# A two-layer hybrid block in fp32: every pair of the up-projection in seven products, its sums of h formed from the transposes, the modulation in single steps

## The chip, the cores and the metric

The kernel runs on one core of one Trainium2 chip. The metric is the device time of one execution in microseconds. The engines have these names in the profile: PE is the matmul engine (PEld its weight loads), DVE the vector engine, ACT the scalar engine, POOL is GpSimd, and SP the engine whose queue issues the DMAs here. SBUF is the on-chip memory in which the kernel keeps its tiles, PSUM the banks into which PE writes. All sizes are fp32: a 128x512 tile is 256 KB.

## What is computed

Two layers on 1024 tokens of width 1024, batch 1. Each layer has a mixer of three parallel branches and an MLP of width 4096. Six vectors from a condition, the modulation, scale and shift the two normalised inputs and gate the two outputs.

```python
cond = jax.nn.silu(c)
for l in range(DEPTH):
    mod = (cond @ w_ada[l] + b_ada[l])[:, None, :]
    sh_m, sc_m, g_m, sh_f, sc_f, g_f = jnp.split(mod, 6, axis=-1)
    h = _rmsnorm(x, norm_g[l, 0]) * (1.0 + sc_m) + sh_m
    y = _hybrid_mixer(h, ...)
    x = x + g_m * _rmsnorm(y, norm_g[l, 1])
    h = _rmsnorm(x, norm_g[l, 2]) * (1.0 + sc_f) + sh_f
    y = jnp.square(jax.nn.relu(h @ w_up[l])) @ w_down[l]
    x = x + g_f * _rmsnorm(y, norm_g[l, 3])
```

The change is in `h @ w_up` (1024x1024 by 1024x4096), in what leads up to it, and in the places at which the modulation is worked out.

## The kernel before

**Products.** Every fp32 operand is split into a high part (fp32r) and a remainder (`split`: a cast on ACT at L199, a subtraction on DVE at L200). A product is three matmuls: high by high (L192), high by low (L193), low by high (L194). The split arrays lie in numbered slots of one tile, named `split` in the profile; fp32 buffers come from an arena, named `arena_f`.

**Layout.** h is kept transposed: features on partitions in eight blocks of 128, tokens along the free dimension, as a high array hh and a low array hl. `B(k, n)` is a quarter of it: four feature blocks (k) by 512 tokens (n). A product of 12 matmuls takes four feature blocks of 128 weights by 512 tokens.

**The up-projection** (`mlp_up`) takes the 32 blocks of 128 hidden features in pairs. Fourteen pairs are done in seven products instead of eight, each 2x2 block problem by sums: the products use B(0,0), B(1,0), B(1,1) and four sums of quarters of h, T0 to T3; the weights are summed alike on POOL and split (`forms`, `cut`), and DVE adds the products up (L316-334). The first four blocks, f = 0 to 3, are done plainly, in 24 matmuls for each half of the tokens, 192 in all. They give the time in which the T sums are formed from hh and hl (`form`): each of the four sums has four blocks, each with two subtractions (L248, L249), an addition (L250) and a split. Three sums are on DVE and T2 on POOL. A later sum needs an earlier one: T1 needs T0, T3 needs T1. Then follow 14 x 7 x 12 = 1176 matmuls. The sums of weights reuse the slots of the second token half of h, one ring of four.

**What comes ahead.** The output projection's last two token tiles, out(6) and out(7), are woven with the second norm of tiles 0 to 5 (`renorm`: a norm whose last addition is on POOL at L596, eight transposes on PE at L604, a cast and a subtraction at L606 and L607). The norms of tiles 6 and 7 are a generator, `late`, that `mlp_up` drains between the halves of its first two plain blocks.

**The down-projection** (`mlp_down`) reads the squared hidden blocks back from memory (d_r) in nine groups of 2, 4, 4, 4, 4, 4, 4, 2 and 4 blocks, with eight token tiles each. In the last group `finish` adds the residual of a token tile and, in layer 0, starts the next layer's norm and transposes (L612).

**The modulation** is worked out in chunks of 128 columns: 512 KB of w_ada, eight multiply-adds of 128x128 on DVE (L535), a matmul with ones (L546), and a small store. A generator, `bg`, is stepped at fixed places: once a pair in up, once a block in down, two chunks a step. It has 56 chunks behind layer 0's mixer and none behind layer 1's.

**Order.** A scheduler with a simulated timeline reorders the instructions when the program is built; on the chip each engine takes its own queue in that order, and the DMAs named above are all issued from SP's queue. So what is written in one place of the code may stand among others in a queue.

## Time and profile before

| | us |
|---|---|
| median of three runs | 2866.52 |
| lowest and highest | 2861.63, 2880.45 |
| the profiled execution | 2878.17 |
| its span, first to last instruction | 2876.5 |
| mean granted clock of PE | 0.946 |

The profiled execution is 11.65 us above the median; the prediction's durations are all from it. In the page, busy time of an engine is the sum of its instructions' durations, and a matmul's duration covers more than its share of a pipelined stream, so a pace is read from counts in a window of full load. "Idle before" is the time in which an engine waited, and the name behind the arrow is what ended it. The granted clock is the share of full speed that PE had. A line of this profile, such as L604, is five lines lower after the change from `mlp_up`'s end on (L609), since the code above it grew.

### The profile page before, as it was taken

The numbers are of one execution on the slowest core, as the hardware profiler recorded it, in microseconds if no ns is written. First come the engines' busy times: TensorE is split into PE (matmuls) and PEld (weight loads), VectorE is DVE, ScalarE is ACT, GpSimd is POOL, SyncE is SP. The second block draws the span as 40 slices with busy tenths as digits, with TensorE's granted clock in tenths as the row PEclk, the third lists the DMA queues.
The fourth block names the chain that finished last, engine by engine and source line by source line (L and its number), as shares of the span: only waits on it lengthen the run. The fifth ranks groups of instructions, "written<-read, shape, count | busy, mean of one in ns | idle before, by whom it ended". The sixth has DMA issues, their size and how long they took to land. (4 is left out here: it accounts for less than half of the span.)

```text
span 2876.5 us, 34698 instructions
## 1 busy us (share of the span) xinstructions
PE 2661.0 (93%) x12578; PEld 2078.7 (72%) x12578; DVE 1747.1 (61%) x3148; ACT 1098.4 (38%) x2105; POOL 665.7 (23%) x532
## 2 busy tenths in 40 slices
PE   5799998999789998999988999999987999999998
PEld 4677776676667776678867877666766788788886
DVE  7767677543878667764365585664448655543435
ACT  5233444544344444212142443454443555621212
POOL 1341244201532220000042113341016432100002
PEclk9899989899899999999998998899998999999999
DMA  6441213312255455643141121132131433541303
GB/s 222 115 132 56 86 59 95 100 58 87 65 165 168 135 164 168 213 155 117 43 138 42 55 83 64 60 110 77 51 118 51 139 114 110 176 149 60 117 30 117
DMA packets 257231, 306.80 MB, mean 107 GB/s; under 512 B 25442, under 2 KB 200740, under 8 KB 257060
## 3 DMA queue, kind: packets, MB, share of 16 engines
q1 hardware_dynamic: 257060, 304.59, 32.9%
q8 instruction: 99, 1.62, 0.2%
q14 instruction: 72, 0.59, 0.1%
HBM read 238.11 MB, written 66.43 MB: 106 GB/s over the span
## 5 line engine op out<-in xcount | busy, mean ns | idle before, releaser
L192 PE MATMUL bank_b<-split 128*128 128x512 f32 (+2 forms) x1840 | 736.1, 400 | 44.1 <-ACT split L199 24.1
L194 PE MATMUL bank_b<-split 128*128 128x512 f32 (+2 forms) x1840 | 716.6, 390 | 7.5 <-DVE split L200 6.5
L193 PE MATMUL bank_b<-split 128*128 128x512 f32 (+2 forms) x1840 | 718.2, 390 | 0.4 <-DVE split L651 0.3
L199 ACT CAST split<-arena_f 128x512 fp32r<-128x512 f32 (+1 forms) x364 | 274.3, 778 | 748.5 <-PE bank_s L193 360.0
L192 PE MATMUL bank_s<-split 128*128 128x512 f32 (+2 forms) x1152 | 455.6, 399 | 29.2 <-ACT split L199 12.6
L193 PE MATMUL bank_s<-split 128*128 128x512 f32 (+2 forms) x1152 | 453.7, 394 | 9.1 <-DVE split L200 5.9
L194 PE MATMUL bank_s<-split 128*128 128x512 f32 (+2 forms) x1152 | 450.3, 391 | 0.0
L192 PEld LDWEIGHTS bank_b<-split 128*128 128x128 f32 x1840 | 358.1, 195 | 125.3 <-ACT split L199 25.8
L194 PEld LDWEIGHTS bank_b<-split 128*128 128x128 f32 x1840 | 356.5, 194 | 79.6 <-DVE split L200 9.3
L193 PEld LDWEIGHTS bank_b<-split 128*128 128x128 f32 x1840 | 358.4, 195 | 68.1 <-issue 4.5
L200 DVE TENSOR_TENSOR split<-arena_f,split 128x512 fp32r<-128x512 f32 (+1 forms) x356 | 334.9, 956 | 111.7 <-ACT split L199 111.5
L375 DVE TENSOR_TENSOR arena_f<-arena_f,bank_s 128x1024 f32<-128x1024 f32 x128 | 155.9, 1218 | 269.8 <-PE bank_s L194 269.8
L192 PEld LDWEIGHTS bank_s<-split 128*128 128x128 f32 (+1 forms) x1152 | 219.4, 191 | 84.5 <-ACT split L199 15.3
L193 PEld LDWEIGHTS bank_s<-split 128*128 128x128 f32 (+1 forms) x1152 | 220.8, 192 | 58.8 <-DVE split L200 9.6
L194 PEld LDWEIGHTS bank_s<-split 128*128 128x128 f32 (+1 forms) x1152 | 220.6, 192 | 44.1 <-issue 1.0
L825 DVE TENSOR_REDUCE nm<-bank_s 128x1 f32<-128x128 f32 (+3 forms) x192 | 141.7, 751 | 125.4 <-PE bank_s L1040 65.2
L826 ACT ACTIVATE arena_f<-bank_s,nm 128x128 f32<-128x128 f32 (+4 forms) x192 | 141.9, 741 | 189.3 <-DVE nm L825 163.9
L535 DVE SCALAR_TENSOR_TENSOR arena_f<-arena_f,cond 128x128 f32<-128x128 f32 x448 | 163.9, 394 | 65.4 <-DMA arena_f<-in_w_ada 28.7
L625 POOL TENSOR_TENSOR arena_f<-arena_f 128x1024 f32<-128x1024 f32 x16 | 43.7, 2731 | 596.9 <-DVE arena_f L624 593.8
L891 PE MATMUL bank_s<-split 32*128 32x512 f32 (+3 forms) x576 | 117.3, 383 | 12.1 <-ACT arena_f L826 9.8
L854 ACT COPY arena_f<-bank_t 128x512 f32<-128x512 f32 (+1 forms) x160 | 86.7, 542 | 104.9 <-PE bank_t L851 94.5
L838 PE MATMUL bank_a<-arena_f 128*64 128x256 f32 (+1 forms) x640 | 108.4, 398 | 13.6 <-ACT arena_f L854 12.1
(277 smaller groups left out, 3286.6 us busy)
## 6 DMA issues: line engine op xcount, KB each, us to landing
arena_f<-in_w_ada SPq DMA_DIRECT2D x80, 512.0 KB
d_r<-arena_f SPq DMA_DIRECT2D x128, 256.0 KB
arena_f<-in_w_down SPq DMA_DIRECT2D x64, 512.0 KB
arena_f<-d_r SPq DMA_DIRECT2D x64, 512.0 KB
arena_f<-in_w_up SPq DMA_DIRECT2D x28, 1024.0 KB
arena_f<-d_x SPq DMA_DIRECT2D x36, 512.0 KB
d_x<-arena_f SPq DMA_DIRECT2D x24, 512.0 KB
arena_f<-in_w_in SPq DMA_DIRECT2D x20, 512.0 KB
```

Of the source, the lines that this page charges most:

```text
L192: mm(out, wh, xh, start=start, stop=False)
L193: mm(out, wh, xl, start=False, stop=False)
L194: mm(out, wl, xh, start=False, stop=stop)
L199: self.nc.scalar.copy(hi, src)
L200: (eng or self.nc.vector).tensor_sub(lo, src, f32(hi))
L375: nc.vector.tensor_add(y[t], y[t], ps)
L535: nc.vector.scalar_tensor_tensor(acc, in0=w[:, k], scalar=self.cond[:, k:k + 1], in1=acc, op0=ALU.mult, op1=ALU.add)
L825: nc.vector.tensor_reduce(nm, S[:, 0:n], axis=AX.X, op=ALU.max, negate=True)
L826: nc.scalar.activation(p[:, 0:n], S[:, 0:n], AF.Exp, bias=nm, accum_out=ls)
L838: nc.tensor.matmul(bk[jj * 64:jj * 64 + 64, 128 * half:256], v[:, 2 * c + jj], e[:, 256:384] if half else e[:, jj * 256:jj * 256 + 256], s ...
L854: nc.scalar.copy(held, ps[:, 0:w])
L891: nc.tensor.matmul(S[mp][:, c0:c1], Q[rw, a, tok], K[rw, b, c0:c1], start=a == b, stop=a == 1 and c1 < n)
```

## The change

All 16 pairs are done in seven products. For the first six (`LEAD`) the two products that need no sum, B(0,0) and B(1,0), run first: they need the tokens 0 to 511 alone. The first of the two is kept in the arena until the pair's other five products. From the seventh pair on, all seven stand together. The plain blocks and `form` go.

The norms of tiles 4 to 7 are `late` now, two steps of it ahead of each lead pair, and the weave ahead has tiles 0 to 3 alone. For tiles 4 to 7, `transp_late` takes the place of `transp8`: POOL adds the high and low parts of the first token half (two additions, L208), PE transposes (L211), and DVE forms the four sums of a tile from the transposes' PSUM, each fp32 sum split at once into its columns of T0 to T3 (four subtractions, L217, and five splits, L230 and L231). The weights of the first six pairs are read a second time for their second part.

A step of the modulation's generator is one chunk instead of two; up has two steps a pair, down one after every second token tile of groups 1 to 6 and after every tile of group 7, and none in groups 0 and 8. In the last group of down in layer 0, the next layer's norm of a tile comes a tile earlier and its transposes one tile earlier, so one deferred norm instead of two is left behind the last tile.

Counts: 24 matmuls of 128x512 fewer in each layer. Three places show what moves in the queues.

DVE in layer 0, before, from the last late norm on (L595 the norm, L607 the remainders of two transposed tiles; L248 to L250 and L200 the sums T and their splits):

```order
L595 SCALAR_TENSOR_TENSOR arena_f<-arena_f,rstd_y_5864 128x1024
L607 TENSOR_TENSOR split<-bank_s,split 128x8x128 x2
L248 TENSOR_TENSOR arena_f<-split 128x512 x4
L249 TENSOR_TENSOR arena_f<-split 128x512 x4
L250 TENSOR_TENSOR arena_f<-arena_f 128x512 x4
L200 TENSOR_TENSOR split<-arena_f,split 128x512
L248 TENSOR_TENSOR arena_f<-split 128x512
```

DVE in layer 0, after, between the norm of the last tile (L600) and the sums of that tile (L217, L231; L307 adds two products, L540 is the modulation's multiply-add):

```order
L600 SCALAR_TENSOR_TENSOR arena_f<-arena_f,rstd_y_5960 128x1024
L231 TENSOR_TENSOR split<-arena_f,split 128x512 x2
L540 SCALAR_TENSOR_TENSOR arena_f<-arena_f,cond 128x128 x4
L307 TENSOR_TENSOR arena_f<-arena_f,bank_b 128x512
L540 SCALAR_TENSOR_TENSOR arena_f<-arena_f,cond 128x128 x7
L217 TENSOR_TENSOR arena_f<-bank_s,arena_f 128x512
L540 SCALAR_TENSOR_TENSOR arena_f<-arena_f,cond 128x128
L217 TENSOR_TENSOR arena_f<-bank_s,arena_f 128x512
L540 SCALAR_TENSOR_TENSOR arena_f<-arena_f,cond 128x128
L231 TENSOR_TENSOR split<-arena_f,split 128x4x128
L217 TENSOR_TENSOR arena_f<-arena_f 128x512 x2
L540 SCALAR_TENSOR_TENSOR arena_f<-arena_f,cond 128x128
```

The sums stand by token tile now, with the modulation's multiply-adds ahead of and among those of the last tile.

PE in layer 0, before: the transposes of the last two tiles stand together, between plain products.

```order
L192 MATMUL bank_b<-split 128x512
L193 MATMUL bank_b<-split 128x512
L604 MATMUL bank_s<-ident,arena_f 128x128 x16
L192 MATMUL bank_b<-split 128x512 x2
L193 MATMUL bank_b<-split 128x512
```

PE in layer 0, after, at the third of four such places, between lead products:

```order
L193 MATMUL bank_b<-split 128x512
L194 MATMUL bank_b<-split 128x512
L211 MATMUL bank_s<-ident,arena_f 128x128 x8
L192 MATMUL bank_b<-split 128x512
L193 MATMUL bank_b<-split 128x512
```

The transposes of tiles 4 to 7 are spread over the lead, a tile at a time.

SP's queue in layer 0, before, at the third and fourth load for the down-projection (L345 reads w_down and the hidden blocks, L520 w_ada, L218 stores hidden blocks):

```order
L520 DMA arena_f<-in_w_ada 128x8x128
L345 DMA arena_f<-in_w_down 128x1024
L520 DMA arena_f<-in_w_ada 128x8x128
L345 DMA arena_f<-in_w_down 128x1024
L520 DMA arena_f<-in_w_ada 128x8x128
L218 DMA d_r_109<-arena_f 128x512
L557 DMA d_mod<-arena_f 1x128
L526 DMA arena_f<-in_b_ada 1x128
L218 DMA d_r_109<-arena_f 128x512
L531 DMA arena_f<-in_norm_g 1x128
L520 DMA arena_f<-in_w_ada 128x8x128
L218 DMA d_r_109<-arena_f 128x512
```

The same place after (L349, L525 and L248 are those three; L644 reads w_in for the next layer):

```order
L349 DMA arena_f<-in_w_down 128x1024
L349 DMA arena_f<-d_r_109 128x1024
L349 DMA arena_f<-in_w_down 128x1024
L349 DMA arena_f<-d_r_109 128x1024
L562 DMA d_mod<-arena_f 1x128
L248 DMA d_r_109<-arena_f 128x512
L531 DMA arena_f<-in_b_ada 1x128
L525 DMA arena_f<-in_w_ada 128x8x128
L644 DMA arena_f<-in_w_in 128x2x128 x2
L525 DMA arena_f<-in_w_ada 128x8x128
L644 DMA arena_f<-in_w_in 128x2x128
L248 DMA d_r_109<-arena_f 128x512
```

Between the third and the fourth load of w_down stands no w_ada now; from the third to the sixth there are three of them where there were six.

```diff
@@ -29,9 +29,9 @@
 OFF = 0, 0, 0.1, 2
 OUTS = (), (0, 1), (2, 3), (4, 5)
 WOW = 16
-LAG = 4
 NVEC = 6
 GROUPS = [2] + [4] * 6 + [2, 4]
+LEAD = 6
 C_Q, C_K, C_V, C_CQ, C_CKV, C_KR, C_Z, C_XBC, C_DT = 0, 256, 512, 768, 1024, 1152, 1184, 1696, 2464
 
 SLOT = 2048
@@ -194,6 +194,37 @@
         mm(out, wl, xh, start=False, stop=stop)
 
 
+    def sums(self):
+
+        return [self.slot(2 * n, 2, 4, 512) for n in range(4)]
+
+    def transp_late(self, x, hT, t):
+
+        nc, F = self.nc, self.F
+        T = self.sums()
+        tok, sl = slice(t * P, t * P + P), slice((t - 4) * P, (t - 3) * P)
+        b = [F.get(4, P) for _ in range(2)]
+        for n in range(2):
+            nc.gpsimd.tensor_add(b[n], *(f32(h[:, n * 4:n * 4 + 4, sl]) for h in hT))
+        ps = self.bank2()
+        for k in range(KD):
+            nc.tensor.transpose(ps[:, k * P:k * P + P], x[:, k * P:k * P + P], self.ident)
+        pv = ps.rearrange("p (n k q) -> p n k q", n=2, q=P)
+
+        def put(n, a, c):
+
+            e = F.get(4, P)
+            nc.vector.tensor_sub(e, a, c)
+            self.split(e, *(T[n][:, m, :, sl] for m in range(2)))
+            return e
+
+        e1 = put(0, pv[:, 0], b[0])
+        e2 = put(1, pv[:, 1], e1)
+        e3 = put(2, e2, b[0])
+        self.split(pv[:, 1], *(h[:, 4:8, tok] for h in hT))
+        e4 = put(3, b[1], e2)
+        F.put(e1, e2, e3, e4, *b)
+
     def split(self, src, hi, lo, eng=None):
 
         self.nc.scalar.copy(hi, src)
@@ -212,91 +243,47 @@
 
         def store(f, hf, t):
 
-            r = F.get(512) if t.tensor is not self.F.t.tensor else t
-            nc.scalar.activation(r, t, AF.Relu)
-            nc.scalar.activation(r, r, AF.Square)
-            dma(self.d_r[l][f, :, half[hf]], r)
-            F.put(r)
-
...
+            nc.scalar.activation(t, t, AF.Relu)
+            nc.scalar.activation(t, t, AF.Square)
+            dma(self.d_r[l][f, :, half[hf]], t)
+            F.put(t)
+
+
+        ring = [tuple(h[:, k, half[1]].rearrange("p (k f) -> p k f", f=P) for h in hT) for k in range(4)]
+        turn = [0]
+
+        def cut(src):
+            r = ring[turn[0] % 4]
+            turn[0] += 1
+            self.split(src, *r)
+            return r
+
+        def forms(i, plain, sums):
+
+            n = 2 * P if sums else P
+            st = F.get(KD, n)
+            dma(st, w_up[:, :, i * 2 * P:i * 2 * P + n])
+            a11, a12 = st[:, 0:4, 0:P], st[:, 4:8, 0:P]
+            if plain:
+                yield cut(a11)
+                yield cut(a12)
+            if sums:
+                a21, a22 = st[:, 0:4, P:2 * P], st[:, 4:8, P:2 * P]
+                s1, s2 = F.get(4, P), F.get(4, P)
+                nc.gpsimd.tensor_add(s1, a21, a22)
+                nc.gpsimd.tensor_sub(s2, s1, a11)
+                yield cut(s2)
+                nc.gpsimd.tensor_sub(a21, a11, a21)
+                yield cut(a21)
+                yield cut(s1)
+                nc.gpsimd.tensor_sub(s2, a12, s2)
+                yield cut(s2)
+                F.put(s1, s2)
+                yield cut(a22)
             F.put(st)
...
         N = FF // (2 * P)
-        parts = self.chain(*(forms(i) for i in range(2, N)))
+        parts = self.chain(*(forms(i, True, False) for i in range(LEAD)), *(forms(i, i >= LEAD, True) for i in range(N)))
         queue = [next(parts) for _ in range(3)]
 
         def product(b):
@@ -310,18 +297,24 @@
             return ps
 
         add = nc.vector.tensor_add
-        for i in range(2, N):
-            f = 2 * i
-            ps, p1 = product(B(0, 0)), F.get(512)
-            nc.scalar.copy(p1, ps)
+        T = [tuple(t[:, a] for a in range(2)) for t in self.sums()]
+        p1 = {}
+
+        def plain(i):
+            ps, p = product(B(0, 0)), F.get(512)
+            nc.scalar.copy(p, ps)
             ps, c = product(B(1, 0)), F.get(512)
-            add(c, p1, ps)
-            store(f, 0, c)
-            ps, u2 = product(part(1)), p1
-            add(u2, p1, ps)
-            ps, u3 = product(part(2)), F.get(512)
+            add(c, p, ps)
+            store(2 * i, 0, c)
+            p1[i] = p
+
+        def sums(i):
+            f, p = 2 * i, p1.pop(i)
+            ps, u2 = product(T[1]), p
+            add(u2, p, ps)
+            ps, u3 = product(T[2]), F.get(512)
             add(u3, u2, ps)
-            ps = product(part(0))
+            ps = product(T[0])
             add(u2, u2, ps)
             c = F.get(512)
             add(c, u3, ps)
@@ -329,9 +322,20 @@
             ps = product(B(1, 1))
             add(u2, u2, ps)
             store(f, 1, u2)
-            ps = product(part(3))
+            ps = product(T[3])
             add(u3, u3, ps)
             store(f + 1, 0, u3)
+
+        for i in range(LEAD):
+            next(late, None)
+            next(late, None)
+            plain(i)
+        self.drain(late)
+        for i in range(N):
+            if i >= LEAD:
+                plain(i)
+            sums(i)
+            next(bg, None)
             next(bg, None)
 
     def mlp_down(self, l, y, bg, finish):
@@ -360,7 +364,6 @@
             rw = []
             for f in fs:
                 rw.append((load(self.d_r[l][f]), load(w_dn[f * P:(f + 1) * P, :])))
-                next(bg, None)
             for t in range(NT):
                 tok = slice(t * P, t * P + P)
                 ps = self.bank2()
@@ -375,6 +378,8 @@
                     nc.vector.tensor_add(y[t], y[t], ps)
                 if last:
                     finish(t)
+                elif g and t % 2 or g == len(GROUPS) - 2:
+                    next(bg, None)
             for (i, _), (k, _) in rw:
                 free.extend((i, k))
 
@@ -1275,7 +1280,10 @@
         self.norm(x, *nxt, u)
         F.put(x)
         yield 1.0
-        self.transp8(u, hT[0], hT[1], t, True)
+        if t < 4:
+            self.transp8(u, hT[0], hT[1], t, True)
+        else:
+            self.transp_late(u, hT, t)
         F.put(u)
         yield 1.0
 
@@ -1303,9 +1311,9 @@
         nxt = self.mod_load(l, 4), self.mod_load(l, 3)
         kept = {}
         self.weave((26, self.chain(out(6, own(6), kept), out(7, own(7), kept))),
-                   (14, self.chain(*(self.renorm(t, dst, nxt, hT) for t in range(6)))))
+                   (9, self.chain(*(self.renorm(t, dst, nxt, hT) for t in range(4)))))
         yield
-        yield from self.chain(*(self.renorm(t, kept, nxt, hT) for t in (6, 7)))
+        yield from self.chain(*(self.renorm(t, dst if t < 6 else kept, nxt, hT) for t in range(4, NT)))
         F.put(g, *nxt)
 
     @staticmethod
@@ -1458,18 +1466,18 @@
                         tail["w"] = list(self.stage_w(I["w_in"][l + 1], self.qk_cols(0), 2))
                 if more and t == NT - 1:
                     tail["w0"] = self.load_w(tail["w"], 2)
-                if more and LAG - 1 < t < NT:
-                    self.transp8(y[t - LAG], hT[0], hT[1], t - LAG)
-                    F.put(y[t - LAG])
+                if more and 2 < t < 7:
+                    self.transp8(y[t - 3], hT[0], hT[1], t - 3)
+                    F.put(y[t - 3])
+                if more and 0 < t <= NT:
+                    self.norm(tail["x"][(t - 1) % 3], *tail["nxt"], y[t - 1], nc.vector if t > NVEC else nc.gpsimd)
                 if t < NT:
                     self.finish(y[t], self.d_x[2 * l], tail["g"], o, t, tail["x"][t % 3], y[t],
                                 hT[0][:, :, t * P:t * P + P])
-                if more and t > 1:
-                    self.norm(tail["x"][(t - 2) % 3], *tail["nxt"], y[t - 2], nc.vector if t > NVEC else nc.gpsimd)
 
             bg = iter(())
             if more:
-                bg = self.mod_stream(self.mod_rows(0, (5,) if l == 0 else (), 128) + self.mod_rows(l + 1, range(6), 128), 2)
+                bg = self.mod_stream(self.mod_rows(0, (5,) if l == 0 else (), 128) + self.mod_rows(l + 1, range(6), 128), 1)
             with self.phase(t=1, b=3):
                 self.mlp_up(l, hT, bg, late)
             with self.phase(t=2, b=2):
@@ -1479,9 +1487,8 @@
                 F.put(tail["g"])
                 if more:
                     finish(NT)
-                    finish(NT + 1)
                     F.put(*tail["nxt"])
-                    for t in range(NT - LAG, NT):
+                    for t in range(4, NT):
                         self.transp8(y[t], hT[0], hT[1], t, True)
                         F.put(y[t])
                         yield
```

60 lines of the change are left out of this document (removed).

## The prediction

> **What bounds the kernel now.** I read the page first, for the busy shares and the chain that ended last.
>
> ```profile
> PE 2661.0 (93%) x12578; PEld 2078.7 (72%) x12578; DVE 1747.1 (61%) x3148; ACT 1098.4 (38%) x2105; POOL 665.7 (23%) x532
> PE 32%; DVE 4%; ACT 1%; DMA 1%; issue 1%; POOL 1%; POOLq 0%; SPq 0%; DVEq 0%; ACTq 0%
> ```
>
> PE is busy for 93% of the span, so time is won either by fewer matmuls or in the places where PE waits or runs slowly. The windows find those places. Their columns are the stretch, its length, busy time and count of PE, weight loads, DVE, ACT and POOL, then the granted clock, the DMA share and GB/s.
>
> ```profile
> 2260.00:2280.00 20.00, 20.00 (x90) 16.57 (x89) 11.75 (x15) 10.27 (x18) 7.77 (x5) 1.00 0.34 117
> 733.00:815.00 82.00, 56.86 (x229) 44.49 (x227) 68.43 (x99) 28.25 (x47) 46.62 (x27) 0.82 0.32 99
> ```
>
> The first row is the up-projection at full speed: 90 matmuls of 128x512 in 20 us, 0.222 us each. The second is a stretch that the change rebuilds, from the last matmul of the output projection to the first product of the pairs, in layer 0. Its ends, and those of layer 1, are in the timeline (start, duration, engine, line, what it works on, idle before it).
>
> ```profile
> 733.63 1.03 PE L604 MATMUL bank_s<-ident,arena_f 128*128 128x128 f32 x8
> 753.50 1.97 PE L604 MATMUL bank_s<-ident,arena_f 128*128 128x128 f32 x8 [3.56 <-POOL arena_f L596]
> 814.88 0.80 PE L192 MATMUL bank_b<-split 128*128 128x512 f32 x1 [10.72 <-ACT split L199]
> 2163.74 1.91 PE L604 MATMUL bank_s<-ident,arena_f 128*128 128x128 f32 x16
> 2234.84 0.50 PE L192 MATMUL bank_b<-split 128*128 128x512 f32 x1 [0.75 <-ACT split L199]
> ```
>
> Layer 0 spends 814.88 - 733.63 = 81.3 us and layer 1 71.1 us on 192 plain matmuls (192 x 0.222 = 42.6) and 24 transposes (about 3). The rest, 35 and 25 us, is waiting and half-speed matmuls. The waits of PE in 733 to 816 (total, times, longest) say on whom:
>
> ```profile
> PE bank_b L192 <- ACT split L199: 16.1, 2, 10.7
> PE bank_s L604 <- POOL arena_f L596: 5.0, 2, 3.6
> PE bank_b L194 <- DVE split L200: 2.9, 2, 2.2
> ```
>
> ACT is named, but only because its cast stands behind a DVE result: DVE makes three of the four sums of h, and is busy 68 of 82 us.
>
> **The lead: price of its parts.** Its durations come from DVE and POOL rows of the same stretch.
>
> ```profile
> 757.69 5.86 DVE L248 TENSOR_TENSOR arena_f<-split 128x512 f32<-128x512 f32 x4
> 763.47 6.86 DVE L249 TENSOR_TENSOR arena_f<-split 128x512 f32<-128x512 f32 x4
> 770.26 4.63 DVE L250 TENSOR_TENSOR arena_f<-arena_f 128x512 f32<-128x512 f32 x4
> 775.41 0.68 DVE L248 TENSOR_TENSOR arena_f<-split 128x512 f32<-128x512 f32 x1
> 776.01 0.68 DVE L200 TENSOR_TENSOR split<-arena_f,split 128x512 fp32r<-128x512 f32 x1
> 756.66 6.34 POOL L248 TENSOR_TENSOR arena_f<-split 128x512 f32<-128x512 f32 x4 [3.22 <-ACT split L606]
> 762.96 5.13 POOL L249 TENSOR_TENSOR arena_f<-split 128x512 f32<-128x512 f32 x3
> 768.06 5.07 POOL L250 TENSOR_TENSOR arena_f<-arena_f 128x512 f32<-128x512 f32 x3
> 790.40 1.27 POOL L249 TENSOR_TENSOR arena_f<-split 128x512 f32<-128x512 f32 x1
> 751.10 2.34 POOL L596 TENSOR_TENSOR arena_f<-arena_f 128x1024 f32<-128x1024 f32 x1 [4.66 <-DVE arena_f L595]
> 749.73 1.28 DVE L595 SCALAR_TENSOR_TENSOR arena_f<-arena_f,rstd_y 128x1024 f32<-128x1024 f32 x1
> 741.59 0.14 DVE L166 TENSOR_SCALAR rs_m<-fs 128x1 f32<-128x1 f32 x1
> 746.21 1.23 DVE L1258 TENSOR_TENSOR arena_f<-arena_f 128x1024 f32<-128x1024 f32 x1
> 756.55 1.22 DVE L607 TENSOR_TENSOR split<-bank_s,split 128x1024 fp32r<-128x1024 f32 x1 [4.04 <-ACT split L606]
> ```
>
> With POOL at rest a DVE operation of 128x512 follows the last after 0.60 us (775.41 to 776.01). The twelve operations from 757.69 to 774.9 took 17.2 us where 12 x 0.60 = 7.2 would do, and POOL worked 16.5 us of that time: each us of POOL cost DVE 10.0 / 16.5 = 0.6 us.
>
> The changed lead has 144 matmuls (six pairs, two products of 12) and 32 transposes. PE alone needs 144 x 0.222 + 4 x 1.03 = 36 us. On DVE, from the same start to the first product with a sum, the order has 36 operations of the T sums (4 tiles x 9), 8 cuts of weights and 6 adds of products, 50 x 0.60 = 30; three norms of 1.28 with a short chain each, 5.0 (an estimate); and the last tile's root, scale and add, 741.59 to 747.44 less an L607 of 1.1 that stands between, 4.7. Together 39.7 us. In layer 0 also 24 of the modulation's multiply-adds stand among them, 0.27 apiece (23 in 6.13 us, row below): 6.5, so 46.2. POOL in the same stretch has 8 new adds of 1.27 and three or four of 2.34: 18.4 us. DVE, not PE, sets the lead.
>
> Bounds: 46 (layer 0) and 40 (layer 1) if POOL costs DVE nothing; 46 + 18 = 64 and 40 + 18 = 58 if DVE stands still whenever POOL works, and beyond that the waits at the head of DVE's queue, of which layer 0 has those for the modulation's weights:
>
> ```profile
> 977.39 0.71 DVE L535 SCALAR_TENSOR_TENSOR arena_f<-arena_f,cond 128x128 f32<-128x128 f32 x1 [6.57 <-DMA arena_f<-in_w_ada]
> 981.50 0.77 PE L192 MATMUL bank_b<-split 128*128 128x512 f32 x1 [3.54 <-DVE arena_f L327]
> 980.00:1000.00 20.00, 18.50 (x69) 14.63 (x70) 12.84 (x26) 9.96 (x18) 2.62 (x3) 0.83 0.50 158
> 1132.06 6.13 DVE L535 SCALAR_TENSOR_TENSOR arena_f<-arena_f,cond 128x128 f32<-128x128 f32 x23 [1.90 <-DMA arena_f<-in_w_ada]
> ```
>
> The multiply-adds are queued ahead of the last tile's T sums, so one such wait of 6.57 delays the first product with a sum in full. I take the measured 0.6: 46.2 + 0.6 x 18.4 + 6.6 = 64 in layer 0, and 39.7 + 11 + 4 for the last tile's chain of row steps = 55 in layer 1 (in layer 0 before, DVE idled 4.04 us for the transposes of tile 7). **The leads give -17 (81.3 to 64) and -16 (71.1 to 55).** Far ends: 46 and 40, or 77 and 66, the full exclusion with two such waits or chains.
>
> The Trainium skill, page "SBUF — State Buffer", section "Who interferes with whom", says that a VectorE instruction with two SBUF inputs and a GpSimd instruction that reads SBUF exclude each other for the whole instruction, while VectorE with one SBUF input does not contend. This speaks against the new adds on GpSimd, and by it only the three of a tile's nine T operations that read PSUM escape. The trace agrees in direction: 17.2 us for 7.2 us of work, 0.6 of POOL's time and not all of it. The full exclusion is the second rival below.
>
> **The other parts.** The remaining main loop has 1200 matmuls where it had 1176: 24 x 0.222 = +5.3 in each layer, **+10.7**; the PE stream as a whole loses 2 x 24. Sixteen transposes and two norms leave the stretch ahead of the lead, 2 x 16 x 0.13 = 4 us in both layers; I take **-2**, between -4 and 0, since out of step with the matmuls part of it lay beside stalls. The second load of 6 x 512 KB of w_up per layer I cost at nothing: the DMA share in the lead was 0.32. If that cover goes, the first cuts come late, which the wide ends hold.
>
> Modulation: per step one chunk instead of two, 32 chunks in the up-projection, the rest between token tiles of the down-projection's middle groups. Where it costs most before is the change from up to down in layer 0.
>
> ```profile
> 1100.00:1120.00 20.00, 17.53 (x77) 13.14 (x76) 16.83 (x31) 10.98 (x15) 0.21 (x1) 1.00 0.66 222
> 1120.00:1140.00 20.00, 17.13 (x70) 13.02 (x70) 11.51 (x39) 5.46 (x7) 1.43 (x7) 0.91 0.45 140
> 1140.00:1160.00 20.00, 9.74 (x36) 5.37 (x34) 17.73 (x48) 8.13 (x13) 0.96 (x5) 0.70 0.73 235
> 1160.00:1180.00 20.00, 19.17 (x76) 13.88 (x77) 15.04 (x31) 4.46 (x7) 0.00 (x0) 0.88 0.88 259
> 2500.00:2520.00 20.00, 16.57 (x67) 13.27 (x66) 15.11 (x15) 14.49 (x18) 0.00 (x0) 0.91 0.93 323
> 1140.00 8.72 DVE L535 SCALAR_TENSOR_TENSOR arena_f<-arena_f,cond 128x128 f32<-128x128 f32 x30 [0.52 <-DMA arena_f<-in_b_ada]
> 1156.09 6.48 SPq L520 DMA_DIRECT2D arena_f<-in_w_ada  x3
> ```
>
> In these 80 us PE did 259 of the 360 matmuls that full speed allows: 101 x 0.222 = 22 us lost. The same place in layer 1, which has no modulation, lost 23 x 0.222 = 5. So 17 us hang on modulation. Between the third and the sixth load of w_down SP now issues three loads of w_ada instead of six, and no run of 30 multiply-adds stands ahead of the splits, because the steps fall singly between token tiles. **I take -12**, half of the 17 for the loads and a part of the rest for the run; bounds -17 and 0, since three loads stay. Inside up I take 0 (-6 to +8): 256 multiply-adds against 240, and a stall like that at 977 is as likely in another place.
>
> The end of layer 0 loses one deferred norm, but tiles 4 to 7 are still transposed after the last matmul, and the wait is DVE's backlog:
>
> ```profile
> 1516.67 1.94 PE L612 MATMUL bank_t<-ident,arena_f 128*128 128x128 f32 x8 [12.29 <-DVE split L615]
> 1503.52 2.79 DVE L595 SCALAR_TENSOR_TENSOR arena_f<-arena_f,rstd_y 128x1024 f32<-128x1024 f32 x1
> ```
>
> One norm of 2.79 less: **-3** (-8 to +3).
>
> **The sum.** -17 - 16 + 10.7 - 2 - 12 + 0 - 3 = -39. The profiled execution took 2878.2 us and stands 11.7 above the median of 2866.5; it goes to 2839, and carried to the median, 2827.
>
> **Rivals.**
> - Leads near DVE's bare work, 52 and 46, since most adds of POOL fall into DVE's own waits: -29 - 25 + 10.7 - 17 = -60, 2806. For it: the T sums of a tile come after its norm, so POOL's work can fall where DVE waits. Against it: 757 to 775.
> - Full exclusion between POOL and DVE: 46 + 18 + 7 = 71 and 40 + 18 + 4 = 62, gains of 10 and 9: -25, so 2841. For it: six of a tile's nine T operations have two SBUF inputs, as all twelve in 757 to 775 have, and the short adds of POOL may fall just there. Against it: the measured 0.6. It is the page's rule, taken at its word.
> - The modulation's loads stay in SP's way at the start of down, so that term is nothing: -27, so 2839.
> - Slower: DVE waits for w_ada in the first six pairs, which have only 60 matmuls (13.3 us) each. Their DVE work is 11 x 0.60 and 16 x 0.27 = 10.9 us; the slack is 2.4, where a full pair of 84 matmuls (18.7 us) had 18.7 - 13.3 = 5.4. A wait of 6.57 then reaches PE with 4 us, and with the half-speed matmuls after it (69 instead of 90 in 980 to 1000, 4.7 us) costs 9. If each of the six pairs in layer 0 has one and the leads are 77 and 66: 6 x 9 - 4 - 5 + 10.7 - 5 = +51, about 2917. With such leads four of these waits make it slower by 1%; with the leads as summed five are needed to lose the whole gain. Against it: of 448 multiply-adds before, 11 waited for w_ada (total and times):
>
> ```profile
>   DMA arena_f<-in_w_ada: 28.7, 11
> ```
>
>
> **How the numbers follow.** About 1% is what a measurement of this kernel can tell from no change: 2838 to 2895 is "the same". Chances: as summed 0.46, with its own range 2814 to 2838; lean leads 0.12; full exclusion 0.24; loads in the way 0.08; slower 0.10. The likeliest case gives 2827. The range reaches from the lean leads with 10 us more from modulation and the end, 2796, to leads near their far ends without a gain at the start of down, 2862; below it lie 3 in 100 and above it 12. Faster by over 1%: 0.44 + 0.12 + 0.03 = 0.59. Slower by over 1%: 0.08. The same: 0.33.
>
> **What would show it.** Right: from the end of the output projection to the first product with T, 64 and 55 us, DVE busy throughout in layer 0, its T operations at more than 0.60 us wherever POOL's adds run; after it 90 matmuls in each 20 us; over 300 of 360 matmuls around the start of down. Wrong: PE waits in the first six pairs for DVE or for w_up; a lead as long as before; a start of down with under 270 matmuls.

## The result, and the profile after

| | us | runs |
|---|---|---|
| before, median | 2863.99 (2860.26 to 2880.45) | 8 |
| after, median | 2845.09 (2842.76 to 2853.57) | 8 |
| ratio | 0.9928, 95% interval 0.9904 to 0.9952 | |
| the same pair measured again, on another occasion | 0.9974, 0.9949 to 1.0 (2861.78 after, 2869.54 before) | 10 and 20 |

The change makes the kernel 0.3 to 0.7% faster by the two measurements; the interval of the second ends at 1.0, which is no change. The forecast was 1.4%, 39 us of the profiled execution. The profiled execution after took 2845.6 us with a span of 2843.7, against 2876.5 before: 33 us less. So the two profiles differ by more than the runs do. This is taken up below.

The page of the profile after begins with the busy shares and the chain that ended last. PE is busy for the same share of a shorter span. The chain is followed back over most of the span here, where before its shares summed to 40%, so the two chains aren't compared:

```profile
PE 2642.4 (93%) x12530; PEld 2063.0 (73%) x12530; DVE 1734.4 (61%) x3163; ACT 1109.0 (39%) x2129; POOL 641.2 (23%) x533
PE 66%; DVE 8%; DMA 6%; issue 4%; ACT 3%; POOL 2%; SPq 0%; POOLq 0%; DVEq 0%; ACTq 0%
```

From here on a product is a single matmul. The timeline gives the ends of the two leads after, as it gave them before (start, duration, engine, line, what it works on, idle before it):

```profile
733.53 1.09 PE L211 MATMUL bank_s<-ident,arena_f 128*128 128x128 f32 x8 [0.80 <-POOL arena_f L601]
800.17 0.80 PE L192 MATMUL bank_b<-split 128*128 128x512 f32 x1
2139.27 1.03 PE L211 MATMUL bank_s<-ident,arena_f 128*128 128x128 f32 x8
2194.20 0.50 PE L192 MATMUL bank_b<-split 128*128 128x512 f32 x1 [2.72 <-ACT split L230]
```

From the transposes behind the output projection to the first product with a sum, layer 0 takes 800.17 - 733.53 = 66.6 us (81.3 before) and layer 1 54.9 (71.1 before). The waits of PE in layer 0's lead (732 to 835; total, times, longest) are no longer those of before:

```profile
PE bank_t L551 <- DVE arena_f L540: 12.7, 1, 12.7
PE bank_b L192 <- ACT split L230: 4.1, 1, 4.1
PE bank_t L551 <- DVE arena_f L559: 3.0, 2, 2.6
```

PE stands 12.7 us in front of a small matmul of the modulation, because the multiply-adds that feed it (L540) are late in DVE's queue; the first product with a sum is behind it. The DVE groups of the stretch 734 to 800 (busy time, mean ns, idle before) show what was counted in the prediction:

```profile
L231 DVE TENSOR_TENSOR split<-arena_f,split 128x512 fp32r<-128x512 f32 x28 | 25.0, 910 | 6.3 <-ACT split L230 6.0 <-PE bank_s L211 0.3
L540 DVE SCALAR_TENSOR_TENSOR arena_f<-arena_f,cond 128x128 f32<-128x128 f32 x24 | 9.9, 418 | 3.7 <-DMA arena_f<-in_w_ada 3.2
L217 DVE TENSOR_TENSOR arena_f<-bank_s,arena_f 128x512 f32<-128x512 f32 x8 | 5.5, 686 | 0.2
L217 DVE TENSOR_TENSOR arena_f<-arena_f 128x512 f32<-128x512 f32 x8 | 5.2, 684 | 0.0
```

The splits from SBUF took 910 ns in the mean, and the sums from PSUM 686. The mean hides two kinds of split: by the timelines of DVE and POOL, of the 26 that start in this stretch the six that ran beside POOL took 1320 ns in the mean and the other 20 took 682. Three sums from PSUM ran beside POOL and took 683. The eight sums with both inputs in SBUF, the last row, took 684, and none of them ran beside POOL. So POOL held up the splits and not the sums from PSUM.

DVE isn't busy throughout either lead. The windows of the two give it 56.75 of 66 us and 42.09 of 55, and in layer 1 PE waits for casts of weights twice, 2.72 us at the row of 2194.20 above and 6.68 here:

```profile
734.00:800.00 66.00, 42.17 (x180) 32.01 (x178) 56.75 (x103) 31.29 (x58) 25.85 (x18) 0.85 0.41 123
2139.00:2194.00 55.00, 40.84 (x178) 32.13 (x177) 42.09 (x75) 31.46 (x58) 20.77 (x11) 0.91 0.31 97
2175.14 0.80 PE L192 MATMUL bank_b<-split 128*128 128x512 f32 x1 [6.68 <-ACT split L230]
```

The change from up to down in layer 0, in the windows that were shown of before:

```profile
1100.00:1120.00 20.00, 17.82 (x78) 13.30 (x77) 14.75 (x37) 10.55 (x13) 0.61 (x3) 1.00 0.89 275
1120.00:1140.00 20.00, 20.00 (x90) 15.65 (x89) 17.58 (x36) 9.48 (x12) 0.82 (x4) 1.00 0.95 306
1140.00:1160.00 20.00, 20.00 (x89) 15.71 (x88) 9.62 (x21) 0.51 (x2) 0.20 (x1) 1.00 0.39 129
1160.00:1180.00 20.00, 20.00 (x89) 15.67 (x89) 12.92 (x12) 8.10 (x10) 0.20 (x1) 1.00 0.46 139
```

PE does 346 products in these 80 us where it did 259. The granted clock is 1.00 throughout.

**Where the time went.** The starts of the first and last products of each part, read off the timeline of PE in each profile, cut an execution into stages. They are found by counting in PE's order, and since a few products of up can stand behind the first of down, a boundary is good to about 1 us. The columns are the first execution of each kernel and a second one of the same program:

| stage, us | before | before, 2nd | after | after, 2nd |
|---|---|---|---|---|
| start to first product of up, layer 0 | 737.0 | 734.7 | 734.4 | 745.0 |
| lead, from that product to the first with a sum | 77.9 | 77.8 | 65.8 | 66.8 |
| the loop behind it | 295.4 | 295.0 | 296.5 | 298.9 |
| last product of up to last of down, layer 0 | 391.9 | 393.3 | 372.6 | 373.2 |
| from there to the 150th product of layer 1 | 52.5 | 52.3 | 59.8 | 60.0 |
| from there to the first product of up, layer 1 | 610.7 | 617.6 | 612.6 | 621.3 |
| lead, layer 1 | 69.4 | 69.5 | 52.5 | 53.5 |
| the loop behind it | 269.4 | 269.3 | 278.0 | 277.1 |
| the rest (down of layer 1, end) | 372.3 | 371.7 | 371.5 | 371.6 |

Seven of the nine stages repeat within 2.4 us, mostly within 1. The first and the sixth, the two mixers, do not, though the change takes only two norms and their 16 transposes out of each mixer's end: over all profiles of this study they lie at 727 to 745 and 611 to 624. The seven give 1528.8 and 1528.9 before, 1496.7 and 1501.1 after: 28 to 32 us less, of which the leads are 27 to 29, the loops a loss of 10 to 12, layer 0's down a gain of 19 to 20, and the stretch behind it a loss of 7 to 8.

### The profile page after: what moved, and what is told of

It is laid out like the page before. It is cut to its first block, busy times and chain, and to the rows that moved or that the text cites. A ratio compares the mean times of both kernels' runs of the same rounds, so it can differ in the third digit from the quotient of the medians.

```text
span 2843.7 us, 34676 instructions
## 1 busy us (share of the span) xinstructions
PE 2642.4 (93%) x12530; PEld 2063.0 (73%) x12530; DVE 1734.4 (61%) x3163; ACT 1109.0 (39%) x2129; POOL 641.2 (23%) x533
## 4 chain that ended last, share of the span: by engine, by line
PE 66%; DVE 8%; DMA 6%; issue 4%; ACT 3%; POOL 2%; SPq 0%; POOLq 0%; DVEq 0%; ACTq 0%
PE bank_b L192 10%; PE bank_b L194 10%; PE bank_b L193 10%; PE bank_s L192 8%; PE bank_s L193 8%; PE bank_s L194 8%; PE bank_a L843 2%; PE bank_s L896 2%; DVE split L231 2%; PE bank_t L856 2%; DMA arena_f<-in_w_up 1%; DVE arena_f L540 1%; DMA d_r<-arena_f 1%; PE bank_a L872 1%; PE bank_b L1189 1%
## 5 line engine op out<-in xcount | busy, mean ns | idle before, releaser
L192 PE MATMUL bank_b<-split 128*128 128x512 f32 (+2 forms) x1824 | 727.4, 399 | 36.1 <-ACT split L230 15.5
L193 PE MATMUL bank_b<-split 128*128 128x512 f32 (+2 forms) x1824 | 709.9, 389 | 2.3 <-DVE split L612 1.9
L194 PE MATMUL bank_b<-split 128*128 128x512 f32 (+2 forms) x1824 | 708.1, 389 | 1.6 <-DVE split L231 1.2
L230 ACT CAST split<-arena_f 128x512 fp32r<-128x512 f32 (+1 forms) x384 | 282.9, 761 | 693.5 <-PE bank_s L193 432.9
L192 PEld LDWEIGHTS bank_b<-split 128*128 128x128 f32 x1824 | 353.1, 194 | 119.3 <-issue 17.4
L231 DVE TENSOR_TENSOR split<-arena_f,split 128x512 fp32r<-128x512 f32 (+1 forms) x384 | 358.1, 950 | 97.7 <-ACT split L230 96.1
L194 PEld LDWEIGHTS bank_b<-split 128*128 128x128 f32 x1824 | 352.7, 193 | 70.9 <-issue 2.5
L193 PEld LDWEIGHTS bank_b<-split 128*128 128x128 f32 x1824 | 353.8, 194 | 67.2 <-issue 4.7
L831 ACT ACTIVATE arena_f<-bank_s,nm 128x128 f32<-128x128 f32 (+3 forms) x192 | 141.9, 741 | 182.7 <-DVE nm L830 151.3
L540 DVE SCALAR_TENSOR_TENSOR arena_f<-arena_f,cond 128x128 f32<-128x128 f32 x448 | 164.5, 396 | 56.4 <-DMA arena_f<-in_b_ada 27.2
L630 POOL TENSOR_TENSOR arena_f<-arena_f 128x1024 f32<-128x1024 f32 x16 | 39.5, 2470 | 479.6 <-DVE arena_f L629 473.7
L246 ACT ACTIVATE arena_f<-arena_f 128x512 f32<-128x512 f32 x128 | 80.8, 632 | 137.0 <-DVE arena_f L320 61.6
L896 PE MATMUL bank_s<-split 32*128 32x512 f32 (+3 forms) x576 | 120.8, 384 | 12.3 <-ACT arena_f L831 10.0
```

Of the source, the lines that this page charges most:

```text
L192: mm(out, wh, xh, start=start, stop=False)
L193: mm(out, wh, xl, start=False, stop=False)
L194: mm(out, wl, xh, start=False, stop=stop)
L230: self.nc.scalar.copy(hi, src)
L231: (eng or self.nc.vector).tensor_sub(lo, src, f32(hi))
L246: nc.scalar.activation(t, t, AF.Relu)
```

## The experiments

Each kernel is the changed one with the edit shown, unless said otherwise. The ratio is to the runs of the kernel before that were made beside it.

**The old end of layer 0 put back.**

```diff
-                if more and 2 < t < 7:
-                    self.transp8(y[t - 3], hT[0], hT[1], t - 3)
-                    F.put(y[t - 3])
-                if more and 0 < t <= NT:
-                    self.norm(tail["x"][(t - 1) % 3], ..., y[t - 1], ...)
+                if more and 3 < t < NT:
+                    self.transp8(y[t - 4], hT[0], hT[1], t - 4)
+                    F.put(y[t - 4])
                 if t < NT:
                     self.finish(y[t], ...)
+                if more and t > 1:
+                    self.norm(tail["x"][(t - 2) % 3], ..., y[t - 2], ...)
...
                     finish(NT)
+                    finish(NT + 1)
```

> The changed kernel with the old end of layer 0 (finish of tile t first, then the norm of tile t - 2, transposes four tiles behind). Theory A: the new end ties a tile's norm to the residual addition of the same tile on POOL, one tile after the other at about 10 us a tile where PE needs 5.3, and this is what costs layer 1's first 150 matmuls 8 us; undone, the time is 8 us below the changed kernel (about 2837) and PE no longer waits 6 us for the L601 of the last tile. Theory B (the prediction): one deferred norm less is worth 3 us; undone, the time is 3 us above (about 2848).

2832.04 us (2829.11 to 2850.69, 4 runs), ratio 0.990 (0.9859 to 0.994). The stretch from the last product of down to layer 1's 150th is 52.4 us, as before the change, where the new end has 59.8. The same edit in four other kernels gave 51.4 to 52.7; the seven profiles with the new end lie at 59.6 to 63.1. The ratio is 0.3 and 0.7% below the changed kernel's two; the stage is the firmer evidence. Theory A holds.

The mechanism is in POOL's rows. With the new end, the residual additions (L630) of the last tiles, and the norms' additions (L601) between them:

```profile
1484.56 2.34 POOL L630 TENSOR_TENSOR arena_f<-arena_f 128x1024 f32<-128x1024 f32 x1
1490.93 3.36 POOL L601 TENSOR_TENSOR arena_f<-arena_f 128x1024 f32<-128x1024 f32 x1 [4.03 <-DVE arena_f L600]
1494.26 2.39 POOL L630 TENSOR_TENSOR arena_f<-arena_f 128x1024 f32<-128x1024 f32 x1
1500.48 3.38 POOL L601 TENSOR_TENSOR arena_f<-arena_f 128x1024 f32<-128x1024 f32 x1 [3.84 <-DVE arena_f L600]
1503.81 2.38 POOL L630 TENSOR_TENSOR arena_f<-arena_f 128x1024 f32<-128x1024 f32 x1
1513.13 3.27 POOL L630 TENSOR_TENSOR arena_f<-arena_f 128x1024 f32<-128x1024 f32 x1 [6.94 <-DVE arena_f L629]
```

With the old end put back:

```profile
1470.23 2.75 POOL L630 TENSOR_TENSOR arena_f<-arena_f 128x1024 f32<-128x1024 f32 x1 [2.46 <-DVE arena_f L629]
...
1486.63 3.52 POOL L630 TENSOR_TENSOR arena_f<-arena_f 128x1024 f32<-128x1024 f32 x1 [4.47 <-DVE arena_f L629]
1490.12 3.35 POOL L601 TENSOR_TENSOR arena_f<-arena_f 128x1024 f32<-128x1024 f32 x1
1493.42 3.38 POOL L630 TENSOR_TENSOR arena_f<-arena_f 128x1024 f32<-128x1024 f32 x1
```

The last down products start at 1469.25 and 1469.92. With the new end the residual additions come one in 9.5 us, each behind the norm of the tile ahead, and that norm waits for its own residual: a chain from tile to tile. The last one ends at 1516.4, 47 us after the last product. With the old end the norm is two tiles behind, no residual waits for the norm of the tile just ahead of it, and the last one ends at 1496.8, 27 us after. PE pays at the transposes. The first two rows are of the changed kernel, at the last transposes written into the loop over tiles and at those of the last tile; the third is of the kernel with the old end:

```profile
1484.65 1.97 PE L617 MATMUL bank_t<-ident,arena_f 128*128 128x128 f32 x8 [14.12 <-POOL arena_f L601]
1521.37 1.97 PE L609 MATMUL bank_s<-ident,arena_f 128*128 128x128 f32 x8 [6.03 <-DVE arena_f L601]
1484.42 1.94 PE L617 MATMUL bank_t<-ident,arena_f 128*128 128x128 f32 x8 [12.30 <-DVE split L620]
```

The long wait is there with either end; the one of 6.03 us is not. In all PE waits 21.2 us in this stage with the new end and 17.0 with the old, 4 of the 7.4 us, and the granted clock of the stage is 0.76 against 0.83.

**The modulation out of the lead.**

```diff
             sums(i)
-            next(bg, None)
-            next(bg, None)
+            for _ in range(0 if i < 3 else 2 if i < 10 else 3):
+                next(bg, None)
```

> The changed kernel with no step of the modulation behind the first three pairs, and three instead of two behind each of the last six, so that none of it stands in the lead. Theory A: in layer 0 the modulation's matmuls with ones and the multiply-adds ahead of the last tile's sums hold the first product with a sum (12.7 us of waiting): the lead falls from 65.8 to 54 us like layer 1's 52.5, and the time by 8 to 11, about 2835. Theory B (lead bound by the T sums, modulation only fills): the lead stays over 62 us and the time within 3 us of 2845.

2857.70 us (2842.43 to 2876.77, 10 runs), ratio 0.9962 (0.9936 to 0.9989). The lead is 62.8 us instead of 65.8, so theory A falls: 12.7 us of waiting went and 3 were gained. Theory B has the lead right, but not the time. The loop behind loses more, 305.9 instead of 296.5; DVE's multiply-adds wait 17.5 us for w_ada in it, 7.6 in the changed kernel. PE's waits in the lead (735 to 802) show what stood behind the one taken away:

```profile
PE bank_b L192 <- ACT split L230: 18.4, 2, 14.3
```

and the chain of that wait is on SP and POOL: the second 1 MB load of the lead is issued at 788.76, and the sums of its weights start when it has landed.

```profile
788.76 0.38 SPq L265 DMA_DIRECT2D arena_f<-in_w_up  x1
794.64 1.26 POOL L273 TENSOR_TENSOR arena_f<-arena_f 128x512 f32<-128x512 f32 x1 [7.69 <-DMA arena_f<-in_w_up]
795.93 0.62 ACT L230 CAST split<-arena_f 128x512 fp32r<-128x512 f32 x1 [6.52 <-POOL arena_f L273]
```

**Stores out of SP's way.** Since stores wait in SP's queue ahead of such loads (18.0 us for ACT in the last experiment's lead), they were issued from ACT's queue, with the modulation as in the last experiment.

```diff
-            dma(self.d_r[l][f, :, half[hf]], t)
+            nc.scalar.dma_start(self.d_r[l][f, :, half[hf]], t)
```

> The changed kernel with the stores of the hidden blocks in up issued from ACT's queue instead of SP's, and the modulation later as in e2. Theory A: with the modulation gone from the lead, layer 0's lead is held by the loads of w_up behind waiting stores in SP's queue (14.3 us of waiting for the first sum of weights); with both out of the way it falls from 62.8 to about 53, like layer 1's. Theory B: the T sums on DVE are the bound and it stays over 60.

2863.38 us (2848.72 to 2878.12, 10 runs), ratio 0.9981 (0.9956 to 1.0007). The lead is 63.0 us: theory A falls again, and theory B has not become right by it, for DVE idles 6.10 us in that place. The waits of SP's queue (735 to 805) name the reason:

```profile
SPq L265 <- DVE split L231: 28.0, 4, 11.7
SPq L265 <- DVE rstd_t L186: 11.9, 1, 11.9
```

The loads wait for their place in the arena. In the program's order, the load for the first pair's second part takes the words that the last tile's sums of h have just left, and the second pair's load stands ahead of it. So it can't start before the sums that it is to be multiplied with are finished, and its 6 us, the weights' sums and the cast come on top. That is read from the trace and the order; a kernel that gives it words of its own was not tried. The loop behind is some 10 us longer than in the run before, with the stores' issue on ACT the only difference.

**Stores on ACT with the old end**, the modulation as in the changed kernel:

> Stores from ACT's queue and the old end of layer 0, modulation as in the changed kernel. Theory A: 8 us from the end and up to 6 from the leads and the loops, in which loads no longer stand behind stores: 12 us below the changed kernel, ratio about 0.988. Theory B: only the end: ratio about 0.991; the issue on ACT costs something in the loops.

2841.05 us (2838.63 to 2850.30, 5 runs), ratio 0.9906 (0.9872 to 0.9941). Leads 66.5 and 55.8, loops 299.5 and 272.0: only the end gains, theory B. Moving the stores gained nothing.

**The modulation's old rhythm.** The steps of two chunks, one step a pair and one a block in down:

```diff
             sums(i)
             next(bg, None)
-            next(bg, None)
...
                 rw.append((load(self.d_r[l][f]), load(w_dn[f * P:(f + 1) * P, :])))
+                next(bg, None)
...
-                elif g and t % 2 or g == len(GROUPS) - 2:
-                    next(bg, None)
...
-                bg = self.mod_stream(..., 1)
+                bg = self.mod_stream(..., 2)
```

> The changed kernel with the modulation as before: two chunks a step, one step a pair, one a block in down. Theory A: the even spread is what made the change from up to down in layer 0 smooth; undone, the stretch from the last up product to the last down product goes from 372.6 back to about 390 us, and the time to about 2862. Theory B: it is the other queue order of the new up-projection that smoothed it; the stretch stays at 373 to 378 us, and the time within 5 us of 2845.

2868.80 us (2865.20 to 2880.73, 10 runs), ratio 1.0012 (0.9993 to 1.003): the whole gain of the change is gone. Layer 0's down is 394.5 us (391.9 and 393.3 before the change, 372.6 with it), and the other stages that repeat lie within 3.3 us of the changed kernel's. In the windows PE does 42 and 56 products where it does 90 and 89:

```profile
1120.00:1140.00 20.00, 11.44 (x42) 6.75 (x40) 15.48 (x44) 7.32 (x12) 0.79 (x4) 0.75 0.63 197
1140.00:1160.00 20.00, 15.01 (x56) 10.31 (x57) 14.64 (x35) 4.71 (x6) 0.41 (x2) 0.74 0.78 254
```

Theory A holds: the spread of the modulation's steps alone is worth these 20 us. The size of a step and its place were changed together and not taken apart.

**The sums' additions on DVE**, in `transp_late`, `nc.gpsimd.tensor_add` made `nc.vector.tensor_add`:

> The changed kernel with the two additions of a tile in the sums of h on DVE instead of POOL. Theory A (POOL costs DVE 0.6 of its time): DVE takes 8 x 0.60 = 4.8 us more in each lead and is spared 0.6 x 10.2 = 6.1; the leads stay within 2 us of 65.8 and 52.5, the time within 4 us of the changed kernel's. Theory B (full exclusion): spared 10.2, so each lead is 5 us shorter and the time 10 us below.

2857.96 us (2849.97 to 2866.17, 10 runs), ratio 0.9944 (0.9919 to 0.9968). Layer 0's lead is 66.8 us (65.8), layer 1's 58.8 (52.5). Theory B falls, and theory A holds for layer 0 alone (the changed kernel's second profile has 66.8 there too): with 10 us of POOL's work gone from each lead, the leads grow by 1 and 6 us, where the additions on DVE cost 4.8. So a lead isn't shortened by the time that POOL costs DVE, neither by all of it nor by 0.6. That fits a lead in which DVE is not always the one that PE waits for.

**More lead pairs**, `LEAD = 8`:

> The changed kernel with eight lead pairs instead of six. Theory A: PE idles 30 us in layer 0's lead and 16 in layer 1's, and 48 more products fill some of it at the price of 4 cuts and 2 adds on DVE (3.6 us): the leads grow by 4 us, the loops behind them shrink by 10.7, the time falls by 13, to about 2832. Theory B: the weights' loads on SP bound the lead, so it grows by the products' 10.7 us or more, and the time stays at 2845 or above.

2853.16 us (2847.21 to 2868.33, 10 runs), ratio 0.9928 (0.9904 to 0.9951). Layer 0: lead 66.1, so the products are hidden, but the loop is 304.2 where 296.5 - 10.7 = 285.8 was expected. Layer 1: lead 69.0, 16 us longer, loop 14.5 shorter. Nothing is gained: theory A falls, and a lead that grows by 10.7 us or more, theory B, is layer 1's alone. In layer 1's lead PE waits twice, 6.6 and 6.8 us, for casts of weights, as in the waits above. In layer 0's loop (807 to 1111) PE waits 18.8 us, mostly for additions of DVE, and DVE's multiply-adds wait 23.9 for w_ada; in the changed kernel the two are 6.6 and 7.6:

```profile
L540 DVE SCALAR_TENSOR_TENSOR arena_f<-arena_f,cond 128x128 f32<-128x128 f32 x220 | 91.2, 433 | 48.5 <-DMA arena_f<-in_w_ada 23.9 <-DMA arena_f<-in_b_ada 18.6 <-issue 4.1
```

**Ten lead pairs and the old end:**

> Ten lead pairs and the old end of layer 0. Theory A: PE's own work in a lead is now 57 us, so layer 1's lead is about 60 and layer 0's about 70, the loops behind are 21 us shorter each, and the old end gives 8: about 2812. Theory B: the leads grow by the 21 us of products, only the end gains: 2837 or above.

2835.82 us (2833.19 to 2838.52, 4 runs), ratio 0.9853 (0.9815 to 0.9891): with that of the kernel that follows, the lowest ratio of the study. The leads grow by 4.6 and 12.6 us, less than the 21 of theory B, but the loops shrink by 12.1 and 27.8 where theory A has 21 each, and the time is theory B's. Leads 70.4 and 65.1, loops 284.4 and 250.2: lead and loop together are 354.8 and 315.3 us, against 362.3 and 330.5 in the changed kernel. PE's waits in layer 1's lead (2147 to 2213) are nearly gone:

```profile
PE bank_b L192 <- ACT split L230: 3.5, 1, 3.5
PE bank_b L192 <- ACT arena_f L305: 1.4, 1, 1.4
```

240 products take 53 us, so PE is now nearer to being the bound of that lead, and most of what is late is covered. Why eight pairs did not do half of this is not settled. With eight, layer 0 loses in the loop by the waits just shown, though with ten DVE still waits 18.2 us for w_ada there and PE 12.3. The two kernels differ in their ends too, and so in the order of what follows.

**The same with the stores on ACT:**

> As e9, with ten lead pairs. Theory A: the loads that held the longer leads (layer 1 65, layer 0 70 us) come in time, each lead shortens toward 60, so 10 to 15 us below the same without it: ratio about 0.981. Theory B: the leads stay at 65 and 70, ratio 0.985.

2828.27 us (2821.00 to 2837.45, 4 runs), ratio 0.9866 (0.983 to 0.9902). Leads 72.8 and 65.8, loops 283.6 and 250.2, as without the stores moved: theory B, and the interval overlaps that of the run above. The profile's 2822 us owe 12 us to a shorter mixer of layer 0 (730.2 against 742.6).

**The old end and the later modulation together:**

> The old end of layer 0 and the later modulation together. Theory A: the two gains lie in different places and add up, about 2827. Theory B: no gain, 2845 to 2850.

2864.85 us (2850.85 to 2882.30, 10 runs), ratio 0.9971 (0.9939 to 1.0003). In the stages the two are there side by side: 52.7 us behind down, as with the old end; lead 62.5 and loop 307.8, as with the later modulation. The time is neither theory's. The seven stages that repeat sum to 1502.0, against 1482.3 with the old end alone, so the later modulation eats the end's gain.

**Each kernel a second time.** The kernel before:

> The kernel before, unchanged, for a second profile. The first one took 2878 us where the median is 2864. Theory A: the 14 us above the median lie in the change from up to down of layer 0, where DMAs decide; here that stretch (last up product to last down product of layer 0) is about 380 us instead of 392. Theory B: they lie elsewhere or are spread, and the stretch is 388 to 394 us again.

2882.96 us, one run, beside 19 of 2864.07 to 2895.97 with a median of 2872.97. Its stages are in the table above: 393.3 in the stretch in question, theory B. The changed kernel:

> The changed kernel itself, beside the other three, and for a second profile. Theory A (the stages are the program's, not the run's): lead of layer 0 64 to 68 us, layer 0 down 371 to 375, last down product to layer 1's 150th product 59 to 61 us; ratio 0.990 to 0.995. Theory B: what the first profile showed was one run's luck, and these three move by more than 4 us.

The three stages held (66.8, 373.2, 60.0); the ratio did not (0.9974), and the 24 us by which this profile is longer than the first are 10.6 in layer 0's mixer and 8.7 in layer 1's. So theory A holds for the stages, and not for the ratio.

## Why the prediction was right and wrong

The measured median of 2845 lies in the range (2796 to 2862) and on the faster side, at half the size forecast; the repeat, 0.9974, is smaller still. Term by term, by the profiles:

| term | predicted | measured |
|---|---|---|
| lead, layer 0 | -17 | -14.7 |
| lead, layer 1 | -16 | -16.2 |
| loops, 24 products more each | +10.7 | +9.7 (1.1 and 8.6) |
| weave ahead of the lead | -2 | hidden in the mixer's scatter |
| up to down, layer 0 | -12 | -19.3 |
| end of layer 0 | -3 | +7.3 |
| sum | -39 | -33 between the first profiles |

**The leads** came out within 3 us in both layers, from DVE rows of another stretch, but not by the account that was given. In layer 0 the busy time is as summed: 56.8 us of DVE, where 46.2 and 11 for POOL were taken. The waiting is not: DVE waits 3.2 us for w_ada, where 6.6 was taken, and 6.0 for casts of weights, for which the prediction had no row. Two chains end within some us of each other, the modulation's small matmul and the first pair's second weights, whose load waits for words of the arena; taking the first away shows the other. In layer 1 the sum had DVE busy for 51 us and it is busy for 42.1; of the rest 7.1 us is its waiting for casts, and PE waits for casts of weights at the rows shown. So the size is right there by luck: POOL's cost was taken too high, and the wait for the weights was missing. Of the signs named beforehand two fail and one holds: DVE is not busy throughout in layer 0, and the loop behind does 1200 products in 296.5 us, 81 in 20 us and not 90; around the start of down PE does 346 of 360.

The 0.6 for POOL's cost does not stand. By the rows of the timelines, DVE's operations beside POOL took 6.8 us more than such operations alone in layer 0's lead (six splits and five others) and 3.2 in layer 1's, where 11 was taken. The reading behind it was loose as well: the 16.5 us of POOL hold waiting of its own, 1.65 us an addition where one alone takes 1.27, and the prediction's 18.4 us of POOL in the lead left out the additions that form the weights, six of about 1.3 us in layer 0.

The page "SBUF — State Buffer" of the Trainium skill, section "Who interferes with whom", was weighed there. The trace agrees on who is hit: beside POOL, sums with one SBUF input took 683 ns, and splits with two took 1320 where 682 is their time alone. Its full exclusion as a price of the lead is not borne out; of POOL's 25.9 us in layer 0's lead, most fell where DVE lost nothing. In layer 1 it was once POOL that stood: one of its additions took 2.87 us, and the three operations of DVE with two SBUF inputs beside it took 687 to 690 ns.

**The end** is the step that failed, and with its sign. It was priced at -3 as "one deferred norm less", by the 2.79 us of that norm; it measured +7.3, and putting it back gave the 7.4 us back. What the edit does besides is to put a tile's norm ahead of the next tile's finish, and this makes two short queues into one long chain, 9.5 us a tile where PE needs 5.3 for 24 products. The order shown ahead of the prediction had no fence on that place.

**Up to down** was mis-sized: 19 us where 12 was taken and 17 was the bound. The bound came from layer 1's loss of 5 us at the same place, taken as a floor; after the change layer 0 loses 14 products there, 3 us.

**From profile to runs.** The prediction carried the sum from the profiled execution to the median unchanged. The stages that repeat give 28 to 32 us; the runs give 19 and 8. Both profiles of the kernel before stand 10 to 14 us above the medians beside them, and their seven stages agree within 0.1 us, so what the shorter runs have less of isn't to be seen in either. The mixers' scatter, 20 us between two profiles of the changed kernel, is as large as the gain, and could hide it in either direction.

The scatter itself can be followed one step further, to the granted clock. Of the 10.6 us by which layer 0's mixer differs between the two profiles of the changed kernel, 9.3 lie in one stretch of 100 matmuls, the same ones in both. The first row is of the first profile, the second of the other:

```profile
428.50:447.10 18.60, 18.60 (x103) 13.84 (x99) 18.45 (x60) 7.48 (x19) 6.41 (x6) 1.00 0.13 33
433.70:461.60 27.90, 27.90 (x105) 20.35 (x101) 21.36 (x63) 8.19 (x20) 7.12 (x7) 0.63 0.13 31
```

PE is busy from end to end in both, and the clock was 1.00 in the one and 0.63 in the other. PE's longest wait in the 20 us ahead of the stretch and in it is 0.6 us in both profiles, so no wait on record tells them apart; why the clock fell stays open. Whole runs go the same way: the ten of the changed kernel on the second occasion reach from 2850.66 us at a mean clock of 0.952 to 2876.28 at 0.940. The median of these clocks is 0.9485, where the eight runs of the first occasion have 0.9535 and the 20 runs of the kernel before on the second 0.9505. So the two ratios differ as the changed kernel's clock does between the two occasions. It stays open whether the mixers are where the ordinary runs differ from the profiles, since only profiled executions show stages.

Of the rivals, the slower one (waits for w_ada in the first six pairs) did not come about: the loop of layer 0 is 1.1 us longer with 24 products more. It can be had, though: with the modulation's steps crowded into later pairs the same loop took 9 us more, and with eight lead pairs 18 more than was expected, with 17.5 and 23.9 us of DVE's waiting for w_ada in place of 7.6. That this waiting is what cost the time is not shown: the loop before the change has 25.1 of it, and PE waits 7.8 us in all there, 6.6 after.

## What to carry to other kernels

When an edit changes which tile's step comes first, write out the chain from one tile to the next and compare its pitch with the pace of the bound engine; counting the work it saves says nothing of that. A wait that is longest in a stretch need not be worth its length: look for what else is due at the same time, and for buffers whose words come free only there. Small background steps spread evenly between tiles cost less than the same steps in bunches (20 us here for 56 chunks), and where the remaining idle time is in a lead, more independent products in it can be worth more than tidying its waits (ten pairs were here, eight were not).

## What the runs showed that was not expected

The two mixers scatter by 18 and 13 us between profiles of programs that run nearly the same work there, while all other stages repeat within 2.4 us for the same program. Where the scatter was followed, it was the granted clock: 18.6 us at 1.00 and 27.9 at 0.63 for the same 100 matmuls, with PE busy throughout. A difference below half a per cent between whole times says little for this kernel; the same difference in a stage is plain.
